# Memory norms inside the first keys' product, later probabilities: a two-layer decoder trunk on one core

## The chip, the cores and the metric

The kernel runs on one core of a Trainium2 chip. The metric is the device time of one execution in microseconds (us); the kernel before is timed at 556.08 us, the median of 3 runs (556.07 to 556.79).

## The reference, cut to what matters

Two layers (`DEPTH = 2`) of width 1024 work on 256 tokens (x) and 256 memory rows (mem), all in float32. Layer 0 mixes tokens with causal windows (`pool_mixer`), layer 1 with masked attention; each layer also lets the tokens attend to the memory with four heads of 64, joins both results in one output projection and ends with an MLP of width 4096.

```python
for i in range(DEPTH):
    u = rms_norm(x, g_mix[i])
    mem_n = rms_norm(mem, g_mem[i])
    ...                       # h = u @ w_in ; tok = pool_mixer(..) or moba_mixer(..) ; qm = last columns of h
    mo = mem_cross_attention(qm, mem_n, w_mem_kv[i], mem_q_gain[i], mem_k_gain[i])
    x = x + jnp.concatenate([tok, mo], axis=-1) @ w_out[i]
    u = rms_norm(x, g_mlp[i])
    x = x + jnp.square(jax.nn.relu(u @ w_ff1[i])) @ w_ff2[i]

def mem_cross_attention(qm, mem_n, w_mem_kv, q_gain, k_gain):
    k, v = jnp.split(mem_n @ w_mem_kv, 2, axis=-1)
    q = rms_norm(qm.reshape(B, S, MEM_HEADS, HEAD_DIM), q_gain)
    k = rms_norm(k.reshape(B, M, MEM_HEADS, HEAD_DIM), k_gain)
    ...
    p = jax.nn.softmax(s, axis=-1).astype(v.dtype)
    o = jnp.einsum('bhsm,bmhd->bshd', p, v)
```

## The kernel before, in words

**Products.** A float32 operand is split into a rounded part `hi` and a rest `lo`; `mm3` (L137 to L140) multiplies them in three matmuls: hi by hi, lo by hi, hi by lo. Weights come in blocks of 512 KB into one pool of seven buffers (`raw`, issued by SyncE in program order, L116). ScalarE makes `hi` (L131 with a gain, L127 without), VectorE makes `lo` (L134, L128). A transfer leaves when the buffer that it takes has been read.

**Stages of layer 0**, in order: the input projection; the memory's keys and values of layer 0, `aK = mem_kv_mm(0, ...)`, eight steps k = 0 to 7 over two accumulators (here called the first keys' product); inside it, at k = 5 (`PLAN['pool']`), the whole of `pooling`: four blocks of pool weights, the window products `band`, which ScalarE and VectorE turn into `d` (L145, L146), and the group products `group`, turned into the first six pieces of `cat`; then `aK1 = mem_kv_mm(1, ...)`, the keys and values of layer 1 (the second keys' product); then the output projection `wout_phase` over eight pieces of `cat`, in the order of `PLAN['wout0']`, four of them on four accumulators and the rest as a tail; then the residual sums and their transposes; then the MLP.

**The memory's part.** After the first keys' product both blocks of mem are loaded and squared (`norm_stats`, L177), and `rsqrt` takes the power on GpSimd (L184). A key block is finished by `head_r` (square L197, sum L199, epsilon L208, power L184), `kn` (L268), `mv` (L269), two transposes (L271) and `mkh`, `mkl`. `mem_scores` makes the scores of one block of 128 queries (L356), their maxima (L360) and exponents (L320), and VectorE divides by the sums (L331). `later` holds back the transposes of the probabilities (L337, L342) by `LAG = 2` steps; `flush` runs what is held; `av_out` (L377) multiplies probabilities and values into pieces 6 and 7 of `cat`. `PLAN['mem0']` says at which k of the second keys' product the steps stand: first key block, second key block, scores of block 0, scores of block 1.

**Order.** The order on each engine is made by a scheduler from dependencies and the program's order, and each engine runs its instructions in that order. Only some stretches are fixed by hand (`manual_schedule`), none of them where the change is. The accumulators are four PSUM banks (`acc`), the other products take turns in four more (`ps`).

Of the kernel before, what the change touches and what calls it, by code (L numbers as in the profile page):

```python
# [35 lines left out]
NWARM = 7  # L36
LAG = 2

PLAN = {'x': 6, 'q': 5, 'bw': 7, 'pool': 5, 'mem0': (2, 4, 6, 6),
        'mem1': (2, 4, 8, 5), 'tok': (5, 7, 8), 'out': 2,  # L40
        'bands': ((0, 2), (1, 1), (3, 5), (4, 4)), 'group': (2, 0, 4), 
        'wout0': (2, 4, 5, 6, 0, 1, 7, 3), 'wout1': (6, 7, 0, 2, 1, 3, 4, 5)}
B0 = P + 16


# [8 lines left out]
def trunk(ctx: ExitStack, tc: tile.TileContext, x, mem, x_t0, x_t, mem_t, small, bands, rope, mask,  # L54
# [13 lines left out]
    def nm(s):  # L68
        uid[0] += 1
        return f"{s}_{uid[0]}"  # L70
# [183 lines left out]

        return [head_r(a[b][:, :MEMW], 4, mem_e64[b], f"mk{b}") for b in range(2)], last_sum[0]

    def mem_kv_finish(l, a, kr, pool):

        kr, sums = kr
        hi = pool.tile([P, 2, S], F32R, tag="mkh", name=nm("mkh"))  # L260
        lo = pool.tile([P, 2, S], F32R, tag="mkl", name=nm("mkl"))
        v = pool.tile([P, 2, MEMW], F32, tag="mv", name=nm("mv"))
        ps = psum("mem_kv_finish")

        def block(b):
            kn = st.tile([P, MEMW], F32, tag="kn", name=nm("kn"))
            with tc.issue_after(sums.ins):
                nc.vector.tensor_tensor(heads(kn), heads(a[b][:, :MEMW]), bcast(kr[b], 4), op=ALU.mult)  # L268
            nc.scalar.activation(v[:, b, :], a[b][:, MEMW:], AF.Copy, scale=mem_r[b])  # L269
            for c in range(2):  # L270
                nc.tensor.transpose(ps[:, c * S + b * P:c * S + b * P + P], kn[:, c * P:(c + 1) * P], ident)  # L271

        def end():
            evac_split(ps.rearrange("p (c t) -> p c t", c=2), hi, lo, mgain[l])
            return hi, lo, v

        return [lambda: block(0), lambda: block(1), end]

    def mem_q(a, b, qT, hold=None):

# [63 lines left out]

        later(back)

    def mem_scores(b, mq, mk, a, pool, nbuf, put):

        ps = [psum("mem_scores") for _ in range(2)]
        for c in range(2):
            for i, (x, y) in enumerate(((0, 0), (0, 1), (1, 0))):
                for j in range(2):
                    rr = slice(j * HD, j * HD + HD)
                    nc.tensor.matmul(ps[j][:, c * S:(c + 1) * S], mq[x][rr, c, b * P:(b + 1) * P], mk[y][rr, c, :],  # L356
                                     start=i == 0, stop=i == 2)
        for j in range(2):
            mx = st.tile([P, 2], F32, tag="mx", name=nm("mx"), bufs=4)
            nc.vector.tensor_reduce(mx, ps[j].rearrange("p (h n) -> p h n", h=2), axis=AX.X, op=ALU.max)  # L360
            nb = st.tile([P, 2], F32, tag="nb", name=nm("nb"), bufs=4)
            nc.vector.scalar_tensor_tensor(nb, mx, -1.0, a[:, j:j + 3:2], op0=ALU.mult, op1=ALU.mult)
            p = pool.tile([P, 512], F32, tag="s", name=nm("s"), bufs=nbuf[0])
            exp_t(pool, [(ps[j][:, c * S:(c + 1) * S], S, a[:, 2 * c + j:2 * c + j + 1], nb[:, c:c + 1])
                         for c in range(2)], p, nbuf[1], lambda t, j=j: put(t, j))

# [10 lines left out]
                        nc.tensor.matmul(o[j * HD:j * HD + HD, cs], vv, pT, start=i == 0, stop=i == n - 1)  # L377
        evac_split(o.rearrange("p (c t) -> p c t", c=2), cat[0][:, c0:c0 + 2, :], cat[1][:, c0:c0 + 2, :])

    def mem_heads(cat, mq, mk, a, pool, nbuf):  # L380

        got = {}

        def scores(b):
            mem_scores(b, mq, mk[:2], a[b], pool, nbuf, lambda t, j: got.__setitem__((b, j), t))

        def gather():
            av_out(cat, 6, [[[(got[b, h % 2][:, (h // 2) * S + kb * P:(h // 2) * S + (kb + 1) * P],
                               mk[2][:, kb, h * HD:(h + 1) * HD]) for kb in range(2)]
                             for b in range(2)] for h in range(4)])  # L390

        return [lambda: scores(0), lambda: scores(1), lambda: later(gather)]
# [132 lines left out]
    with tc.tile_pool(name="l0", bufs=1) as lp:  # L525
# [111 lines left out]
            evac_split(ps.rearrange("p (c t) -> p c t", c=2), cat[0][:, co:co + 2, :], cat[1][:, co:co + 2, :])  # L637

        wpool = {}
        mid_hi = []  # L640

        def pooling():
            for b in range(2):
# [10 lines left out]
                band_pair(c0, c1)  # L654
            for co in PLAN['group']:
                group_pair(co)
            mid_hi.append(last_hi[0])


        mgain = []  # L660
        for l in range(2):
# [1 line left out]
            nc.vector.scalar_tensor_tensor(g, sm[:, MQG + l:MQG + l + 1], 8.0, sm[:, MKG + l:MKG + l + 1],  # L663
                                           op0=ALU.mult, op1=ALU.mult)
            mgain.append(g)
        aK = mem_kv_mm(0, [(PLAN['pool'], pooling)])
        mem_r, mem_e64 = [], []
        after = mid_hi[0]
        for b in range(2):
            raw = load_raw(mem[b * P:(b + 1) * P, :])  # L670
            ms = norm_stats(raw[:, 0, :], f"mem{b}", after)
            mem_r.append(rsqrt(ms, f"mem{b}"))
            mem_e64.append(scaled(ms, 64.0 * EPS, f"mem{b}"))
        kr = mem_kv_norm(aK)
        steps = []

        def mem_keys(i):
# [1 line left out]
                steps.extend(mem_kv_finish(0, aK, kr, lp))  # L679
            steps[i]()  # L680
            if i == 1:
                steps.extend(mem_heads(cat, mq, steps[2](), mqa, lp, (2, 4)))

        aK1 = mem_kv_mm(1, list(zip(PLAN['mem0'], [lambda: mem_keys(0), lambda: mem_keys(1),
                                                   lambda: steps[3](), lambda: steps[4]()])))
        steps[5]()
        flush()
        steps = mem_kv_finish(1, aK1, mem_kv_norm(aK1), mkp)
        mk1 = [step() for step in steps][2]
        x1T = big_t("x1T")  # L690
        after_mix(wout_phase(0, PLAN['wout0'], cat, PSC), x1T)


    x2T = big_t("x2T")
# [234 lines left out]
```

## Time and profile before

| | |
|---|---|
| median of 3 runs | 556.08 us |
| the profiled execution | 557.27 us |
| its span, first to last instruction | 555.5 us |
| TensorE (PE) busy | 545.8 us, 98% |
| VectorE (DVE) busy | 386.5 us, 70% |
| ScalarE (ACT) busy | 357.5 us, 64% |
| granted TensorE clock | 1.000 |

The span and every row below come from one profiled execution, whose time outside the span is 1.8 us. PE is TensorE's matrix products, DVE VectorE, ACT ScalarE, POOL GpSimd, SP SyncE. A row of the timeline gives start, length and work; the bracket at its end is the idle time ahead of it on that engine and who ended it. Products overlap: one of 512 columns is shown 0.39 us long, while the next starts 0.23 us after it. So a wait of TensorE is best read from the starts.

### The profile page before, as it was taken

The numbers are of one execution on the slowest core, as the hardware profiler recorded it, in microseconds if no ns is written. First come the engines' busy times: TensorE is split into PE (matmuls) and PEld (weight loads), VectorE is DVE, ScalarE is ACT, GpSimd is POOL, SyncE is SP. The second block draws the span as 40 slices with busy tenths as digits, with TensorE's granted clock in tenths as the row PEclk, the third lists the DMA queues.
The fourth block names the chain that finished last, engine by engine and source line by source line (L and its number), as shares of the span: only waits on it lengthen the run. The fifth ranks groups of instructions, "written<-read, shape, count | busy, mean of one in ns | idle before, by whom it ended". The sixth has DMA issues, their size and how long they took to land.

```text
span 555.5 us, 8204 instructions
## 1 busy us (share of the span) xinstructions
PE 545.8 (98%) x2883; PEld 456.8 (82%) x2883; DVE 386.5 (70%) x765; ACT 357.5 (64%) x658; POOL 43.7 (8%) x57
## 2 busy tenths in 40 slices
PE   8999899999999999999999999999999999999997
PEld 5888687888888888888888876888888888888885
DVE  5897978584864945848979988565858477485462
ACT  5888967756566566565769579757664665656510
POOL 0102100000000000000013365300000000000000
PEclk9999999999999999999999999999999999999999
DMA  8989674355737538458571444342574483663401
GB/s 283 353 255 345 229 239 136 105 196 213 226 129 250 178 138 291 124 181 264 168 233 65 158 152 151 116 152 77 183 272 137 167 281 101 225 208 140 145 0 76
DMA packets 46712, 101.94 MB, mean 184 GB/s; under 512 B 3664, under 2 KB 11600, under 8 KB 46672
## 3 DMA queue, kind: packets, MB, share of 16 engines
q1 hardware_dynamic: 46528, 101.42, 55.5%
q8 instruction: 22, 0.36, 0.3%
q14 instruction: 18, 0.15, 0.1%
q10 hardware_dynamic: 144, 0.01, 0.0%
HBM read 100.37 MB, written 1.05 MB: 183 GB/s over the span
## 4 chain that ended last, share of the span: by engine, by line
PE 85%; ACT 6%; DVE 4%; DMA 2%; POOL 2%; issue 1%; SPq 1%; ACTq 0%
PE step L462 18%; PE acc L139 16%; PE acc L138 16%; PE acc L140 16%; PE step L465 10%; PE acc L462 3%; ACT hi L131 2%; PE av_out L377 2%; ACT s L320 1%; PE acc L465 1%; DMA raw<-in_w_in_pool_dram 1%; DVE lo L134 1%; DMA raw<-in_w_mem_kv_dram 1%; POOL r L184 1%; PE exp_t L337 1%; PE transpose L157 1%
## 5 line engine op out<-in xcount | busy, mean ns | idle before, releaser
L131 ACT ACTIVATE hi<-raw,sm 128x512 fp32r<-128x512 f32 (+1 forms) x212 | 148.4, 722 | 53.3 <-PE acc L140 25.6
L134 DVE SCALAR_TENSOR_TENSOR lo<-raw,sm,hi 128x512 fp32r<-128x512 f32 x212 | 150.3, 749 | 19.0 <-ACT hi L131 18.2
L127 ACT ACTIVATE hi<-raw 128x512 fp32r<-128x512 f32 (+1 forms) x152 | 93.9, 630 | 73.8 <-PE acc L140 65.6
L138 PE MATMUL acc<-hi,hh 128*128 128x512 f32 x256 | 99.9, 390 | 0.0
L140 PE MATMUL acc<-hi,hl 128*128 128x512 f32 x256 | 99.8, 390 | 0.0
L139 PE MATMUL acc<-lo,hh 128*128 128x512 f32 x256 | 99.8, 390 | 0.0
L128 DVE TENSOR_TENSOR lo<-raw,hi 128x512 fp32r<-128x512 f32 (+1 forms) x152 | 96.4, 692 | 3.6 <-ACT hi L127 3.5
L446 DVE TENSOR_TENSOR r<-step,c 128x256 f32<-128x256 f32 x56 | 23.6, 421 | 98.6 <-ACT c L445 98.6
L140 PEld LDWEIGHTS acc<-hi,hl 128*128 128x128 f32 x256 | 48.1, 188 | 10.0
L138 PEld LDWEIGHTS acc<-hi,hh 128*128 128x128 f32 x256 | 48.1, 188 | 9.5
L139 PEld LDWEIGHTS acc<-lo,hh 128*128 128x128 f32 x256 | 48.1, 188 | 9.4
L462 PE MATMUL step<-x3T,hi 128*128 128x512 f32 x224 | 51.9, 389 | 0.0
L462 PE MATMUL step<-x1T,hi 128*128 128x512 f32 x224 | 51.9, 389 | 0.0
L462 PEld LDWEIGHTS step<-x3T,hi 128*128 128x128 f32 x224 | 42.0, 188 | 8.7
L462 PEld LDWEIGHTS step<-x1T,hi 128*128 128x128 f32 x224 | 42.0, 188 | 8.7
L445 ACT ACTIVATE c<-step 128x256 f32<-128x256 f32 x56 | 21.2, 379 | 19.5 <-PE step L465 19.5
L138 PE MATMUL acc<-hi,x2T 128*128 128x512 f32 x80 | 32.2, 403 | 0.0
L140 PE MATMUL acc<-hi,x2T 128*128 128x512 f32 x80 | 31.2, 391 | 0.0
L139 PE MATMUL acc<-lo,x2T 128*128 128x512 f32 x80 | 31.2, 391 | 0.0
L465 PEld LDWEIGHTS step<-x3T,lo 128*128 128x128 f32 x224 | 27.8, 192 | 0.5
L465 PEld LDWEIGHTS step<-x1T,lo 128*128 128x128 f32 x224 | 27.8, 192 | 0.5
L465 PE MATMUL step<-x3T,lo 128*128 128x256 f32 x224 | 28.0, 283 | 0.0
(152 smaller groups left out, 758.9 us busy)
## 6 DMA issues: line engine op xcount, KB each, us to landing
raw<-in_w_ff_dram SPq DMA_DIRECT2D x128, 512.0 KB, 4.8
raw<-in_w_out_dram SPq DMA_DIRECT2D x16, 512.0 KB, 4.9
raw<-in_w_in_moba_dram SPq DMA_DIRECT2D x24, 256.0 KB, 4.5
raw<-in_w_mem_kv_dram SPq DMA_DIRECT2D x8, 512.0 KB, 5.4
raw<-in_w_in_moba_dram SPq DMA_DIRECT2D x8, 512.0 KB, 5.0
raw<-in_w_in_pool_dram SPq DMA_DIRECT2D x6, 512.0 KB, 7.1
raw<-in_w_in_pool_dram SPq DMA_DIRECT2D x4, 256.0 KB, 4.5
xr<-in_x_dram SPq DMA_DIRECT2D x2, 512.0 KB, 7.5
```

Of the source, the lines that this page charges most:

```text
L127: nc.scalar.activation(hi, raw, AF.Copy)
L128: nc.vector.tensor_tensor(lo, raw, hi.bitcast(F32), op=ALU.subtract)
L131: last_hi[0] = nc.scalar.activation(hi[:, :m], raw[:, :m], AF.Copy, scale=g)
L134: nc.vector.scalar_tensor_tensor(lo, raw, g, hi.bitcast(F32), op0=ALU.mult, op1=ALU.subtract)
L138: nc.tensor.matmul(o, a[0], b[0], start=start, stop=False)
L139: nc.tensor.matmul(o, a[0], b[1], start=False, stop=False)
L140: nc.tensor.matmul(o, a[1], b[0], start=False, stop=stop)
L377: nc.tensor.matmul(o[j * HD:j * HD + HD, cs], vv, pT, start=i == 0, stop=i == n - 1)
L445: nc.scalar.activation(c, zs[i][:, S:], AF.Copy)
L446: nc.vector.tensor_tensor(z[:, i, :], zs[i][:, :S], c, op=ALU.add)
L462: nc.tensor.matmul(o, pieces[k][0][:, n * P:(n + 1) * P], t[2][:, k, :, :], start=k == 0, stop=False)
L465: nc.tensor.matmul(o[:, :S], pieces[k][1][:, n * P:(n + 1) * P], t[0][:, k, :], start=False, stop=k == NKC - 1)
```

## The change

The two blocks of mem are loaded and squared inside the first keys' product, at k = 4 (`mstat`), ahead of `pooling`, instead of after it. The steps of the first keys move from k = 2, 4, 6, 6 to k = 3, 3, 5, 5 of the second keys' product. Up to five held transposes may wait (`lag[0] = 5`), so that probabilities and values run between the pieces of the output projection, ahead of its pieces 1, 2 and 3 (`probs0`). The probabilities of block 1 stay in the buffers of `hhi` and `hlo` (`home`). The second keys are finished in two parts: `kn` and `mv` ahead of the output projection, the transposes after `av_out` (`apart`). The output projection takes the two pieces of `av_out` last.

```diff
-PLAN = {'x': 6, 'q': 5, 'bw': 7, 'pool': 5, 'mem0': (2, 4, 6, 6),
+PLAN = {'x': 6, 'q': 5, 'bw': 7, 'pool': 5, 'mstat': 4, 'mem0': (3, 3, 5, 5), 'probs0': (1, 2, 3),
...
-        'wout0': (2, 4, 5, 6, 0, 1, 7, 3), 'wout1': (6, 7, 0, 2, 1, 3, 4, 5)}
+        'wout0': (2, 4, 5, 0, 1, 3, 6, 7), 'wout1': (6, 7, 0, 2, 1, 3, 4, 5)}
...
-        ps = psum("mem_kv_finish")
+        ps = None if apart else psum("mem_kv_finish")
+        kns = []
...
             nc.scalar.activation(v[:, b, :], a[b][:, MEMW:], AF.Copy, scale=mem_r[b])
+            kns.append(kn)
+            if not apart:
+                turn(b)
+
+        def turn(b):
+            nonlocal ps
+            ps = ps or psum("mem_kv_finish")
             for c in range(2):
-                nc.tensor.transpose(ps[:, c * S + b * P:c * S + b * P + P], kn[:, c * P:(c + 1) * P], ident)
+                nc.tensor.transpose(ps[:, c * S + b * P:c * S + b * P + P], kns[b][:, c * P:(c + 1) * P], ident)
...
-        return [lambda: block(0), lambda: block(1), end]
+        return [lambda: block(0), lambda: block(1)] + [lambda: turn(0), lambda: turn(1)] * apart + [end]
...
-            p = pool.tile([P, 512], F32, tag="s", name=nm("s"), bufs=nbuf[0])
+            if home:
+                p = pool.tile([P, 2, TOK], F32, tag=home[j], name=nm("s"))[:, 0, :512]
+            else:
+                p = pool.tile([P, 512], F32, tag="s", name=nm("s"), bufs=nbuf[0])
...
-        aK = mem_kv_mm(0, [(PLAN['pool'], pooling)])
         mem_r, mem_e64 = [], []
-        after = mid_hi[0]
-        for b in range(2):
-            raw = load_raw(mem[b * P:(b + 1) * P, :])
-            ms = norm_stats(raw[:, 0, :], f"mem{b}", after)
-            mem_r.append(rsqrt(ms, f"mem{b}"))
-            mem_e64.append(scaled(ms, 64.0 * EPS, f"mem{b}"))
+
+        def mem_stats():
+            for b in range(2):
+                raw = load_raw(mem[b * P:(b + 1) * P, :])
+                ms = norm_stats(raw[:, 0, :], f"mem{b}")
+                mem_r.append(rsqrt(ms, f"mem{b}"))
+                mem_e64.append(scaled(ms, 64.0 * EPS, f"mem{b}"))
+
+        aK = mem_kv_mm(0, [(PLAN['mstat'], mem_stats), (PLAN['pool'], pooling)])
...
+        lag[0] = 5
         aK1 = mem_kv_mm(1, list(zip(PLAN['mem0'], [lambda: mem_keys(0), lambda: mem_keys(1),
                                                    lambda: steps[3](), lambda: steps[4]()])))
         steps[5]()
-        flush()
-        steps = mem_kv_finish(1, aK1, mem_kv_norm(aK1), mkp)
-        mk1 = [step() for step in steps][2]
+        steps = mem_kv_finish(1, aK1, mem_kv_norm(aK1), mkp, True)
+        steps[0](), steps[1]()
+        mk1 = []
+
+        def gather():
+            flush()
+            mk1.extend([step() for step in steps[2:]][2])
+
         x1T = big_t("x1T")
-        after_mix(wout_phase(0, PLAN['wout0'], cat, PSC), x1T)
+        after_mix(wout_phase(0, PLAN['wout0'], cat, PSC,
+                             list(zip(PLAN['probs0'], [lambda: flush(2), lambda: flush(2), gather]))), x1T)
+        lag[0] = LAG
```

The scheduler turns this into changes of order, shown at three places. In each row stand the line, the operation and output <- inputs.

First ScalarE, in the first keys' product, from the split of step k = 4 on. `raw_453` holds the weights of k = 4 and 5, `raw_600` those of k = 6 and 7, `raw_469` to `raw_487` are the pool weights, `d` comes from the bands. Before:

```order
L131 ACTIVATE hi_455<-raw_453,sm 128x512
L127 ACTIVATE hi_471<-raw_469 128x512
L127 ACTIVATE hi_477<-raw_475 128x512
L127 ACTIVATE hi_483<-raw_481 128x512
L127 ACTIVATE hi_489<-raw_487 128x256
L131 ACTIVATE hi_590<-raw_453,sm 128x512
L131 ACTIVATE hi_602<-raw_600,sm 128x512
L131 ACTIVATE hi_612<-raw_600,sm 128x512
L145 ACTIVATE d_402<-band_493 128x2x256
L145 ACTIVATE d_402<-band_506 64x256
L145 ACTIVATE d_402<-band_516 128x2x256
```

Of the change (`raw_455` and `raw_466` are mem, `raw_491` to `raw_509` the pool weights, `raw_622` the weights of k = 6 and 7):

```order
L131 ACTIVATE hi_477<-raw_453,sm 128x512
L177 ACTIVATE junk_457,m_458<-raw_455 128x1024
L177 ACTIVATE junk_468,m_469<-raw_466 128x1024
L127 ACTIVATE hi_493<-raw_491 128x512
L127 ACTIVATE hi_499<-raw_497 128x512
L145 ACTIVATE d_402<-band_515 128x2x256
L127 ACTIVATE hi_505<-raw_503 128x512
L127 ACTIVATE hi_511<-raw_509 128x256
L145 ACTIVATE d_402<-band_528 64x256
L145 ACTIVATE d_402<-band_538 128x2x256
L131 ACTIVATE hi_612<-raw_453,sm 128x512
L131 ACTIVATE hi_624<-raw_622,sm 128x512
```

The two squares stand ahead of the pool weights, and the split of k = 5 (`hi_590` before, `hi_612` now) has moved from ahead of the three evacuations of the bands to behind them.

Second TensorE, from the last band product to the first group products (`acc_407` and `acc_408` are the first keys' accumulators). Before:

```order
L611 MATMUL band_516<-bw_254,hlo 128x128
L138 MATMUL acc_407<-hi_590,mth 128x512
L139 MATMUL acc_407<-lo_591,mth 128x512
L140 MATMUL acc_407<-hi_590,mtl 128x512
L138 MATMUL acc_408<-hi_590,mth 128x512
L139 MATMUL acc_408<-lo_591,mth 128x512
L140 MATMUL acc_408<-hi_590,mtl 128x512
L138 MATMUL acc_407<-hi_602,mth 128x512
L139 MATMUL acc_407<-lo_603,mth 128x512
L138 MATMUL group_539<-d_402,hi_477 128x256
```

Of the change:

```order
L624 MATMUL band_538<-bw_254,hlo 128x128
L138 MATMUL acc_407<-hi_612,mth 128x512
L138 MATMUL acc_408<-hi_612,mth 128x512
L138 MATMUL group_561<-d_402,hi_499 128x256
L138 MATMUL group_576<-d_402,hi_493 128x256
L139 MATMUL group_576<-d_402,hi_493 128x256
```

Between bands and groups there were eight products, now two, and both need the split of k = 5.

Third the end of the second keys, on VectorE up to `kn` of both blocks. Before:

```order
L324 RECIPROCAL inv_825<-sums_822 128x2
L128 TENSOR_TENSOR lo_1041<-raw_1034,hi_1040 128x512
L331 TENSOR_SCALAR s_821<-s_821,inv_825 128x256 x2
L199 TENSOR_REDUCE ss_899<-sq_897 128x4
L134 SCALAR_TENSOR_TENSOR lo_1047<-raw_1044,sm,hi_1046 128x512
L208 TENSOR_SCALAR sst_901<-ss_899,s_642 128x4
L268 TENSOR_TENSOR kn_909<-acc_660,r_895 128x256
L268 TENSOR_TENSOR kn_914<-acc_661,r_903 128x256
```

Of the change:

```order
L340 TENSOR_SCALAR s_790<-s_790,inv_794 128x256 x2
L333 RECIPROCAL inv_806<-sums_803 128x2
L199 TENSOR_REDUCE ss_844<-sq_842 128x4
L340 TENSOR_SCALAR s_802<-s_802,inv_806 128x256 x2
L208 TENSOR_SCALAR sst_846<-ss_844,s_464 128x4
L199 TENSOR_REDUCE ss_852<-sq_850 128x4
L128 TENSOR_TENSOR lo_1037<-raw_1034,hi_1036 128x512
L208 TENSOR_SCALAR sst_854<-ss_852,s_475 128x4
L270 TENSOR_TENSOR kn_861<-acc_660,r_848 128x256
L270 TENSOR_TENSOR kn_864<-acc_661,r_856 128x256
```

`kn` of the second keys stands behind all four scaled probabilities (`s_752` to `s_802`) as before; two splits fewer stand between them. On TensorE of the change, from the transposes of the last probabilities on:

```order
L346 MATMUL exp_t_930<-ident,s_790 128x128 x4
L346 MATMUL exp_t_937<-ident,s_802 128x128 x3
L138 MATMUL acc_870<-hi_874,cat_401 128x512
L139 MATMUL acc_870<-lo_875,cat_401 128x512
L140 MATMUL acc_870<-hi_874,cat_401 128x512
```

`acc_870`, the third accumulator of the output projection, is the bank of the second keys' `acc_660`; its first product now follows the transposes of the probabilities at once, where before `av_out` and the second keys' transposes stood between.

## Rows read from the trace of the kernel before

**Rows 1.** The page's part 1: busy time, share of the span, instructions of each engine.

```profile
PE 545.8 (98%) x2883; PEld 456.8 (82%) x2883; DVE 386.5 (70%) x765; ACT 357.5 (64%) x658; POOL 43.7 (8%) x57
```

**Rows 2.** Stretches: length, busy PE, PEld, DVE, ACT, POOL, clock, DMA share, GB/s.

```profile
52.00:66.00 14.00, 12.07 (x71) 9.20 (x71) 12.87 (x30) 13.05 (x28) 1.47 (x2) 1.00 0.83 298
78.00:100.00 22.00, 22.00 (x105) 17.83 (x104) 14.30 (x25) 15.17 (x26) 0.00 (x0) 1.00 0.60 191
```

**Rows 3.** Timeline of TensorE, 51 to 66 us: start, length, work, [idle before <- releaser].

```profile
51.76 0.39 PE L140 MATMUL acc<-hi,mtl 128*128 128x512 f32 x1
52.56 0.44 PE L271 MATMUL mem_kv_finish<-ident,kn 128*128 128x128 f32 x2 [0.41 <-DVE kn L268]
...
58.68 0.38 PE L356 MATMUL mem_scores<-mkh,mqh 64*128 64x256 f32 x2
59.28 0.39 PE L356 MATMUL mem_scores<-mkl,mqh 64*128 64x256 f32 x2 [0.21 <-DVE mkl L149]
...
63.41 0.39 PE L140 MATMUL acc<-hi,mtl 128*128 128x512 f32 x1
65.11 0.63 PE L337 MATMUL exp_t<-ident,s 128*128 128x128 f32 x4 [1.31 <-DVE s L331]
```

**Rows 4.** Timeline of TensorE, 39 to 47 us, bands to the end of the groups.

```profile
39.18 0.45 PE L611 MATMUL band<-bw,hlo 128*128 128x128 f32 x3
...
40.04 0.45 PE L138 MATMUL acc<-hi,mth 128*128 128x512 f32 x1
...
41.94 0.40 PE L138 MATMUL group<-d,hi 128*128 128x256 f32 x2
...
46.97 0.40 PE L140 MATMUL acc<-hi,mtl 128*128 128x512 f32 x1
```

**Rows 5.** Timeline of ScalarE, 34 to 74 us.

```profile
34.62 1.97 ACT L127 ACTIVATE hi<-raw 128x512 fp32r<-128x512 f32 x4
...
39.44 1.40 ACT L145 ACTIVATE d<-band 128x512 fp32r<-128x512 f32 x3 [1.01 <-PE band L611]
...
43.39 1.34 ACT L131 ACTIVATE hi<-raw,sm 128x512 fp32r<-128x512 f32 x2 [1.72 <-DMA raw<-in_w_mem_kv_dram]
...
48.65 1.06 ACT L177 ACTIVATE junk<-raw 128x1024 bf16<-128x1024 f32 x1
...
49.70 0.39 ACT L197 ACTIVATE sq<-acc 128x256 f32<-128x256 f32 x1
...
73.34 0.47 ACT L269 ACTIVATE mv<-acc,r 128x256 f32<-128x256 f32 x1 [0.75 <-DVE kn L268]
```

**Rows 6.** Timeline of VectorE, 53 to 80 us.

```profile
53.50 0.42 DVE L268 TENSOR_TENSOR kn<-acc,r 128x256 f32<-128x256 f32 x1 [1.00 <-POOL r L184]
...
61.00 1.28 DVE L360 TENSOR_REDUCE mx<-mem_scores 128x2 f32<-128x512 f32 x2
...
66.19 1.41 DVE L134 SCALAR_TENSOR_TENSOR lo<-raw,sm,hi 128x512 fp32r<-128x512 f32 x2
...
71.55 0.22 DVE L208 TENSOR_SCALAR sst<-ss,s 128x4 f32<-128x4 f32 x1
...
75.60 4.08 DVE L134 SCALAR_TENSOR_TENSOR lo<-raw,sm,hi 128x512 fp32r<-128x512 f32 x6
```

**Rows 7.** Timeline of GpSimd, 52 to 68 us.

```profile
52.46 1.01 POOL L184 TENSOR_TENSOR r<-sst,mhalf 128x4 f32<-128x4 f32 x1
66.36 1.44 POOL L184 TENSOR_TENSOR r<-sst,mhalf 128x4 f32<-128x4 f32 x1 [12.89 <-DVE sst L208]
```

**Rows 8.** DMA issues at 15.9, 28.4 and 33.1 us: count, KB each, us to landing.

```profile
raw<-in_mem_t_dram SPq DMA_DIRECT2D x1, 256.0 KB, 8.5
...
raw<-in_w_pool_pad_dram SPq DMA_DIRECT2D x1, 256.0 KB, 3.4
...
raw<-in_w_mem_kv_dram SPq DMA_DIRECT2D x1, 512.0 KB, 3.5
```

More of the change, by code (lines that the diff above doesn't have):

```diff
@@ L255, in mem_kv_norm, with mem_kv_finish @@
         return [head_r(a[b][:, :MEMW], 4, mem_e64[b], f"mk{b}") for b in range(2)], last_sum[0]
-    def mem_kv_finish(l, a, kr, pool):
+    def mem_kv_finish(l, a, kr, pool, apart=False):
         kr, sums = kr
@@ L345, in exp_t, with mem_scores @@
         later(back)
-    def mem_scores(b, mq, mk, a, pool, nbuf, put):
+    def mem_scores(b, mq, mk, a, pool, nbuf, put, home=None):
         ps = [psum("mem_scores") for _ in range(2)]
@@ L378, in av_out, with mem_heads @@
         evac_split(o.rearrange("p (c t) -> p c t", c=2), cat[0][:, c0:c0 + 2, :], cat[1][:, c0:c0 + 2, :])
-    def mem_heads(cat, mq, mk, a, pool, nbuf):
+    def mem_heads(cat, mq, mk, a, pool, nbuf, home=None):
         got = {}
         def scores(b):
-            mem_scores(b, mq, mk[:2], a[b], pool, nbuf, lambda t, j: got.__setitem__((b, j), t))
+            mem_scores(b, mq, mk[:2], a[b], pool, nbuf, lambda t, j: got.__setitem__((b, j), t), home if b else None)
         def gather():
@@ L639, in trunk @@
         wpool = {}
-        mid_hi = []
         def pooling():
@@ L656, in pooling @@
                 group_pair(co)
-            mid_hi.append(last_hi[0])
         mgain = []
@@ L681, in mem_keys @@
             if i == 1:
-                steps.extend(mem_heads(cat, mq, steps[2](), mqa, lp, (2, 4)))
+                steps.extend(mem_heads(cat, mq, steps[2](), mqa, lp, (2, 4), ('hhi', 'hlo')))
+        lag[0] = 5
         aK1 = mem_kv_mm(1, list(zip(PLAN['mem0'], [lambda: mem_keys(0), lambda: mem_keys(1),
```

## The prediction

> **What bounds the kernel now.** I read the page's busy times first: TensorE works 98% of the span [rows 1]. So its arithmetic stands, and a change of order can only take away or add waits of TensorE. The stretches say where: from 52 to 66 us it is busy 12.07 of 14 us, while ScalarE and VectorE are nearly full with 13.05 and 12.87; from 78 us on it is never idle and the other two have room [rows 2]. Whatever TensorE loses ahead of 78 us therefore comes out at the end unshortened.
>
> Next I read TensorE's own timeline, by starts. Back to back, a product of 512 columns follows the last after 0.23 us, one of 256 after 0.12: the 42 group products take 46.97 - 41.94 = 5.03 us [rows 4]. Against these spacings TensorE loses three pieces in the stretch that the change touches [rows 3]: 52.56 - 51.76 - 0.23 = 0.57 us for `kn` of the first keys, 59.28 - 58.68 - 0.12 = 0.48 for `mkl`, and 65.11 - 63.41 - 0.23 = 1.47 for the first scaled probabilities. Together 2.5 us. That is all there is to win.
>
> **The change part by part.** All of it is counted from the order on each engine of the changed kernel with lengths of rows of before. Up to 34.62 us, where the split of k = 4 is done, both orders agree.
>
> *Squares moved, 2 x 1.05 us.* A square holds ScalarE from 48.65 to 49.70 [rows 5]. Two of them leave the full stretch and go to where ScalarE has idle time of 1.01 and 1.72 us [rows 5]. Their two VectorE operations each and their powers on GpSimd go along, beside other work, and cost TensorE nothing. The loads of mem go past the four pool weights and the weights of k = 6, 7 on SyncE's queue. The first now takes the place of the pool weights at 28.4 us, and with the bytes ahead of it I put its landing between 3.5 and 6 us later (a lone block of its size took 3.5 [rows 8]), so before ScalarE wants it at 34.62. The weights of k = 6, 7 wait for the buffer of the first square: 34.62 + 1.2 = 35.8 instead of 33.1, landing at 39.3 by the same 3.5; wanted at 42.2 (below). So far the move is free.
>
> *The wait that the move makes.* ScalarE runs in order. After the squares (to 36.7) it splits two pool blocks at 0.52 each (four, the last half as wide, in 1.97 less the overlap [rows 5]) and is ready at 37.8. The next in its order is the first `d`, which needs the last band products. These start on TensorE at 39.18, behind step k = 4 [rows 4], and nothing moves them: `d` starts at 39.44 as now [rows 5]. Behind it stand two pool blocks (0.83 us) and two more pieces of `d`; the three pieces take 1.40 less an overlap of 0.1 [rows 5]. So the split of k = 5 starts at 39.44 + 1.30 + 0.83 = 41.57, and is to be seen 0.76 later, at 42.33 (0.73 long [rows 5], and a hop). TensorE wants it at 40.04, when the bands are done [rows 4]: **a new wait of 2.29 us**. Before, that split ran ahead of the bands' evacuations. TensorE then has two products, to 42.79, and the groups need the last piece of `d`, which now stands behind the split of k = 6: 41.57 + 2 x 0.61 (two splits in 1.34 [rows 5]) + 0.4 = 43.2, **0.41 more**. Groups begin at 43.2 instead of 41.94, and with only 2 of 8 products done ahead of them; TensorE is 2.70 us late.
>
> *First keys, scores, first probabilities.* Groups to 48.23, then ten products of k = 5, 6 and three of k = 7 (13 x 0.23): the first keys' square starts at about 51.4 and, with the 4.2 us from square to second `kn` of now (49.70 [rows 5] to 53.92 [rows 6]), the second `kn` is there at 55.6. TensorE has 34 products first, to 56.05: the wait of 0.57 is gone, with 0.45 to spare. Transposes and two steps bring it to 59.3. VectorE does five splits at 0.67 (six in 4.08 [rows 6]) and `mkl` after 55.6, ready at 59.7: 0.2 us of the 0.48 stay, counting the pair that needs only `mkh`. Scores to 61.05, then 24 products that now stand between scores and probabilities, to 66.6; VectorE has the maxima from 55.6 + 9 x 0.67 = 61.6 on and the first probabilities at 65: the wait of 1.47 is gone. This part does what it says. `home` costs nothing: `hhi` and `hlo` were last read by the bands. The order of the pieces of `wout0` changes no count.
>
> *Second keys.* On TensorE the transposes of the probabilities end at 66.6 + 15 x 0.11 (a group of four is 0.63 long less an overlap of 0.2 [rows 3]) + 6 x 0.23 = 69.65. Then comes the third accumulator, in the bank that the second keys' `mv` must empty; `av_out`, which covered that before, comes later. VectorE took 71.55 - 61.00 = 10.55 us from the first maxima to the second keys' last epsilon, with hardly a break [rows 6]; up to the first of the two, four splits (2.6) and one sum (0.3) less stand there now, 7.6 us: 69.2. Then a power on GpSimd (1.01 [rows 7], with hops 1.1), `kn` (0.42 [rows 6]) and `mv` (0.47 [rows 5]): 71.3. **A new wait of 1.65 us.** Bounds: another power took 1.44, at 66.36, beside splits of VectorE [rows 6, 7], which makes 2.1; and the twelve splits of VectorE on this path at 0.60 instead of 0.67 make 0.85. I take the middle, since at 69.2 VectorE waits for the power soon after. What follows (`av_out`, second transposes) has its inputs early.
>
> On GpSimd's 1.44 us the Trainium skill (SBUF — State Buffer, section "SBUF: two separate sides") says that GpSimd and VectorE lock one shared port pair, for a whole instruction when VectorE reads two SBUF inputs. The splits at 66.19 are such instructions and the trace agrees with 1.44 against 1.01 [rows 6, 7]; by the rule the power would be long here too, and the sum 0.4 us larger.
>
> *The sum.* New 2.29 + 0.41 + 1.65, gone 0.57 + 0.28 + 1.47: 4.35 - 2.32 = +2.0 us. The profiled execution of 557.27 us would become 559.3; it lies 1.2 above the median of the runs shown, so the median goes from 556.08 to **558.1**. The bounds of the last wait alone give 557.3 to 558.5.
>
> **The rivals.** *The wait at the second keys is hidden.* If VectorE is faster on this path (this count has it busy nearly without a break from 42 to 71 us), or TensorE loses more on the way, the third accumulator is free in time and only 2.70 - 2.32 = 0.4 us are left: 556.5, up to 557.1 with half of it. For it: it hangs on a chain of some 30 us; against: four powers and evacuations in a row, none of which can overlap.
>
> *Not slower: the bands end earlier.* It hangs on one place: when the first `d` can start. All that I count behind it, on ScalarE, VectorE and TensorE alike, moves with it one for one, down to the 37.8 at which ScalarE is ready. If the bands' last products ran ahead of step k = 4 on TensorE, `d` would start 1.64 us earlier and the time would be 558.1 - 1.6 = 556.5; from a `d` at 38.5 on it is no longer slower by what can be measured. Only with the hidden second wait on top, 1.65 less, is it faster, 554.8. Against it: both orders have the bands' last products behind k = 4, and TensorE reaches them unhindered at 39.18 [rows 4].
>
> *Slower still: mem lands late.* Loads issued into a full queue took up to 8.5 us [rows 8]. So late, mem would be there at 36.9; two squares and two pool blocks then end at 40.1 instead of 37.8, the first `d` slips by 0.7 and the weights of k = 6, 7 by 2.3, to 41.6, just in time. Some 0.7 to 1 us more: 559.0.
>
> **How the numbers follow.** The forecast 0.57; the hidden second wait 0.23; bands earlier 0.12, of which 0.06 with the second wait hidden too; late mem 0.08. The range for 8 in 10 runs from 556.4 (just under the two cases at 556.5) to 559.1; outside it lie the faster case and what goes beyond late mem. A measurement here can tell about 0.2%, 1.1 us, from no change: faster than 555.0 has 0.06, within 0.2% 0.23 + 0.06 = 0.29, and slower than 557.2 has 0.57 + 0.08 = 0.65.
>
> **What would show it.** In the changed kernel's trace TensorE should wait about 2.3 us for ScalarE's split of weights at 40 us, behind the bands; then 0.4 for a `d`; nothing for `kn` and for the first probabilities; 0.2 for `mkl`; and 0.9 to 2.1 us for `mv` of the second keys at about 70 us. From the second piece of the output projection on it should be as full as before. If the first wait is under 1 us I am wrong about the order's worth; if the waits stand and the time is still below 557, the later stages give something back that I count as nothing.

## The result and the profile after

The changed kernel takes 559.97 us (median of 4 runs, 559.92 to 559.98), the kernel before 556.21 in the same comparison: a ratio of 1.0066, 95% interval 1.0053 to 1.0079. It is slower, as forecast, but by 3.76 us and not by 2.0, and 559.97 lies above the range of 556.4 to 559.1. The profiled execution took 559.98, with a span of 557.9.

The page's busy times answer [rows 1], and the two stretches answer [rows 2] (columns as there):

```profile
PE 547.0 (98%) x2883; PEld 457.8 (82%) x2883; DVE 387.1 (69%) x765; ACT 357.8 (64%) x658; POOL 42.9 (8%) x57
```

```profile
52.00:66.00 14.00, 13.91 (x79) 11.23 (x79) 13.15 (x30) 11.13 (x24) 2.03 (x2) 1.00 0.68 231
78.00:100.00 22.00, 22.00 (x131) 17.81 (x129) 15.37 (x26) 14.22 (x24) 0.00 (x0) 1.00 0.51 161
```

From 52 to 66 us TensorE is now busy 13.91 of 14 us, against 12.07: of the three waits ahead of `kn`, `mkl` and the first probabilities only a part of the one for `mkl` is left (below), and ScalarE has fallen from 13.05 to 11.13. The loss must stand elsewhere. TensorE's list of waits from 24 to 110 us (total, times, longest) has two new long ones:

```profile
PE acc L138 <- ACT hi L131: 2.1, 1, 2.1
PE acc L138 <- ACT mv L271: 1.4, 1, 1.4
PE group L138 <- ACT d L145: 0.3, 1, 0.3
```

TensorE's timeline behind the bands answers [rows 4]; here every row counts by its start:

```profile
38.68 0.45 PE L624 MATMUL band<-bw,hlo 128*128 128x128 f32 x3
...
39.43 0.27 PE L624 MATMUL band<-bw,hlo 128*128 128x128 f32 x1
41.77 0.73 PE L138 MATMUL acc<-hi,mth 128*128 128x512 f32 x2 [2.06 <-ACT hi L131]
42.78 0.79 PE L138 MATMUL group<-d,hi 128*128 128x256 f32 x2 [0.28 <-ACT d L145]
43.38 0.41 PE L139 MATMUL group<-d,hi 128*128 128x256 f32 x1
43.59 0.41 PE L140 MATMUL group<-d,lo 128*128 128x256 f32 x1
...
45.94 0.31 PE L140 MATMUL group<-d,lo 128*128 128x256 f32 x1
46.09 0.28 PE L138 MATMUL group<-d,hi 128*128 128x256 f32 x1
46.20 0.28 PE L139 MATMUL group<-d,hi 128*128 128x256 f32 x1
...
49.32 0.40 PE L139 MATMUL acc<-lo,mth 128*128 128x512 f32 x1
```

The wait stands where the forecast put it. But look at the products after it: up to 45.94 a group product follows the last after 0.21 us, from 46.09 on after 0.12. The 42 of them take 49.32 - 42.78 = 6.54 us instead of 5.03. The stretches' clock column (third from the right) says why:

```profile
40.00:42.00 2.00, 0.23 (x1) 0.24 (x2) 2.00 (x5) 2.00 (x6) 0.00 (x0) 1.00 0.99 354
42.00:44.00 2.00, 1.72 (x7) 1.28 (x7) 1.94 (x5) 1.95 (x5) 0.00 (x0) 0.65 1.03 398
44.00:46.00 2.00, 2.00 (x12) 2.00 (x11) 2.00 (x4) 1.32 (x3) 0.00 (x0) 0.50 1.03 382
46.00:48.00 2.00, 2.00 (x19) 2.00 (x19) 0.73 (x3) 1.36 (x3) 0.00 (x0) 1.00 0.94 363
```

TensorE is busy for only 0.23 us between 40 and 42 us. Behind that the granted clock falls to 0.50, the 1.2 GHz level, and stays there until 46 us; the 0.65 belongs to a stretch that holds both levels. The kernel before kept 1.00 there:

```profile
42.00:44.00 2.00, 2.00 (x19) 2.00 (x18) 0.32 (x1) 0.61 (x1) 0.00 (x0) 1.00 1.04 398
44.00:46.00 2.00, 2.00 (x19) 2.00 (x18) 1.82 (x3) 1.98 (x5) 0.00 (x0) 1.00 1.06 401
```

The rest of TensorE's timeline, at the places of [rows 3]:

```profile
56.82 0.39 PE L140 MATMUL acc<-hi,mtl 128*128 128x512 f32 x1
57.06 0.60 PE L280 MATMUL mem_kv_finish<-ident,kn 128*128 128x128 f32 x4
...
60.36 0.38 PE L366 MATMUL mem_scores<-mkh,mqh 64*128 64x256 f32 x2
60.83 0.39 PE L366 MATMUL mem_scores<-mkl,mqh 64*128 64x256 f32 x2
...
67.68 0.39 PE L140 MATMUL acc<-hi,cat 128*128 128x512 f32 x1
67.91 1.03 PE L346 MATMUL exp_t<-ident,s 128*128 128x128 f32 x8
68.70 0.48 PE L138 MATMUL acc<-hi,cat 128*128 128x512 f32 x1
...
70.16 0.93 PE L346 MATMUL exp_t<-ident,s 128*128 128x128 f32 x7
72.51 0.50 PE L138 MATMUL acc<-hi,cat 128*128 128x512 f32 x1 [1.42 <-ACT mv L271]
```

`kn` and the first probabilities come 0.24 and 0.23 us behind the product ahead of them, which is no wait. `mkl` still costs 60.83 - 60.36 - 0.12 = 0.35. Eight transposes took 0.79, so seven end the work at 70.85, and the third accumulator starts at 72.51: 1.66 us lost.

ScalarE around the first wait, for [rows 5]:

```profile
34.13 1.04 ACT L177 ACTIVATE junk<-raw 128x1024 bf16<-128x1024 f32 x1
...
35.29 1.06 ACT L177 ACTIVATE junk<-raw 128x1024 bf16<-128x1024 f32 x1
...
38.94 0.60 ACT L145 ACTIVATE d<-band 128x512 fp32r<-128x512 f32 x1 [1.45 <-PE band L624]
39.43 0.93 ACT L127 ACTIVATE hi<-raw 128x512 fp32r<-128x512 f32 x2
40.26 0.84 ACT L145 ACTIVATE d<-band 64x256 fp32r<-64x256 f32 x2
41.00 1.33 ACT L131 ACTIVATE hi<-raw,sm 128x512 fp32r<-128x512 f32 x2
42.35 0.38 ACT L145 ACTIVATE d<-band 64x256 fp32r<-64x256 f32 x1
```

The squares run at 34.13 and 35.29 without a wait, so mem is there in time. ScalarE then idles 1.45 us in front of the first `d`, while the split that TensorE will miss stands two pool blocks and two `d` behind it, at 41.00.

**A measure for what follows.** The time from the start to the first band product moves from one execution to the next, in these profiles from 28.46 to 29.40 us, and so do short waits in the second layer. Where kernels are compared by trace, I take the stretch from the first band product to the first memory scores of the second layer. Its two ends, before and then after:

```profile
29.22 0.97 PE L607 MATMUL band<-bw,hhi 128*128 128x256 f32 x4
...
288.53 0.38 PE L356 MATMUL mem_scores<-mkh,mqh 64*128 64x256 f32 x2
```

```profile
28.72 0.97 PE L620 MATMUL band<-bw,hhi 128*128 128x256 f32 x4
...
291.42 0.38 PE L366 MATMUL mem_scores<-mkh,mqh 64*128 64x256 f32 x2
```

It is 288.53 - 29.22 = 259.31 us before and 291.42 - 28.72 = 262.70 after: +3.39. Each of these values is that of one profiled execution.

### The profile page after: what moved, and what is told of

It is laid out like the page before. It is cut to its first block, busy times and chain, and to the rows that moved or that the text cites. A ratio compares the mean times of both kernels' runs of the same rounds, so it can differ in the third digit from the quotient of the medians.

```text
span 557.9 us, 8199 instructions
## 1 busy us (share of the span) xinstructions
PE 547.0 (98%) x2883; PEld 457.8 (82%) x2883; DVE 387.1 (69%) x765; ACT 357.8 (64%) x658; POOL 42.9 (8%) x57
## 4 chain that ended last, share of the span: by engine, by line
PE 84%; ACT 7%; DVE 5%; DMA 1%; issue 1%; POOL 1%; SPq 1%; ACTq 0%; DVEq 0%
PE step L475 18%; PE acc L139 16%; PE acc L138 16%; PE acc L140 16%; PE step L478 10%; PE acc L475 3%; ACT s L329 2%; DVE lo L134 2%; ACT hi L131 2%; PE acc L478 1%; PE av_out L390 1%; DMA raw<-in_w_in_pool_dram 1%; PE transpose L157 1%; ACT hi L127 1%; POOL r L184 1%
```

## The experiments

My theory after the result, **A**: the order makes both waits as forecast, and the rest is the clock, which falls behind the first wait. The rival, **B**: the group products are slow for a reason of their own, such as late operands or splits beside them. The experiments ran in three groups on three chips, each beside the kernel before: its medians were 556.44 us (e1_fill to e4_stats6), 556.55 (e5_after to e8_ahead) and 556.39 (e9_fill to e12_only). Each ratio is against the kernel before of the same group.

**The wait filled (e1_fill).** Ten products of a zero tile behind the bands, in an accumulator that is empty then (it is the one that the second keys' product takes next; the lines that pass it on are left out):

```
             for c0, c1 in PLAN['bands']:
                 band_pair(c0, c1)
+            kv1.extend([accum(), accum()])
+            for _ in range(NFILL):
+                nc.tensor.matmul(kv1[0], warm[:, :P], warm, start=True, stop=True)
```

> The changed kernel with ten products of a zero tile (128x512, bf16, the tile of the warm-up) put on TensorE right behind the band products, in an accumulator that is empty then. They fill the 2.1 us in which TensorE waits there for the split of k = 5; the wait for the split itself, and every other engine's order, stay. Theory A (the idle time costs twice: the forecast left out that the granted clock falls behind it, to 0.50 from 44 to 46 us): the clock reads 1.00 from 40 to 48 us, the 42 group products take about 5.0 us instead of 6.54, the two products of k = 5 take 0.23 each, and the time falls by 1.75 us to 558.2 (557.9 to 558.5). Theory B (the group products are slow for another reason: their operands come late, or they compete for a memory with splits that now run beside them): the clock or not, they still take about 6.5 us and the time stays at 559.9 to 560.1.

Measured 559.46 us, ratio 1.0056 (1.0043 to 1.0069). Two stretches of its trace:

```profile
42.00:44.00 2.00, 1.72 (x9) 0.90 (x8) 1.94 (x5) 1.95 (x4) 0.00 (x0) 1.00 1.04 395
44.00:46.00 2.00, 2.00 (x19) 2.00 (x18) 2.00 (x4) 2.00 (x4) 0.00 (x0) 1.00 1.07 386
```

The clock stays at 1.00 and the groups take 48.60 - 43.46 = 5.14 us, with the same splits beside them. B falls. The stretch measure is 261.40, 1.30 under the changed kernel and +2.09 over the kernel before, which is the forecast's sum of 2.0. My 1.75 was too much: it counted the pair of products of k = 5 as slow, but that pair is 0.73 us long in both traces, and the groups start 14.06 us behind the first band in both, since they wait for `d` anyway. The time of 558.2 was missed too: this profile reaches the bands 0.68 us later, and it came from another chip than the result.

**The norms' move undone (e2_late).** The two squares go behind the pooling again:

```
-        aK = mem_kv_mm(0, [(PLAN['mstat'], mem_stats), (PLAN['pool'], pooling)])
+        aK = mem_kv_mm(0, [(PLAN['pool'], pooling)])
+        mem_stats()
...
-                ms = norm_stats(raw[:, 0, :], f"mem{b}")
+                ms = norm_stats(raw[:, 0, :], f"mem{b}", mid_hi[0])
```

> The changed kernel with the one move of the memory's norms undone: the squares stand behind the pooling again, as in the kernel before; the keys' and scores' new places and the probabilities between the output projection's products stay. Theory A: no wait of TensorE behind the bands, the clock 1.00 throughout, groups 5.0 us, which is 2.1 + 0.3 + 1.75 = 4.2 us back; of that about 0.4 is lost to kn of the first keys (squares late again, transposes one step later than before) and up to 1 to a longer wait at the second keys, whose chain on VectorE cannot be pulled forward as far as TensorE: 556.7 (556.0 to 557.5). Theory B (the lost time has nothing to do with the norms' place or with the idle behind it): 558.2 or more.

Measured 556.67 us, ratio 1.0010 (1.0001 to 1.0019), 259.08 by the stretch. No wait behind the bands, clock 1.00. So the whole loss hangs on the norms' move. What is left of the change is worth little either way: 0.1% more time, 0.23 us less by the stretch. It ends the wait for `kn`, shortens the one for the probabilities from 1.31 to 0.62, and makes a new one of 0.95 at the second keys. The 0.4 for `kn` did not come; the 0.62 for the probabilities was not expected.

**The norms' move alone (e3_only).** The kernel before, with its squares taken to step 4 of the first keys' product:

```
-        aK = mem_kv_mm(0, [(PLAN['pool'], pooling)])
...
+        aK = mem_kv_mm(0, [(PLAN['mstat'], mem_stats), (PLAN['pool'], pooling)])
```

> The kernel before with the one move of the memory's norms into the first keys' product; all else as before. Theory A: TensorE waits 2.1 and 0.3 us behind the bands and the clock falls to about 0.5 for some 3.5 us, as in the changed kernel (+4.2); the waits for kn (0.57) and part of mkl (0.3) go, the wait for the first scaled probabilities stays at 1 to 1.5, and there is none at the second keys: 556.2 + 4.2 - 0.9 - 0.2 = 559.3 (558.6 to 559.8), slower than before although it makes but one of the two new waits. Theory B: the wait alone, without the clock, 557.5.

Measured 560.28 us, ratio 1.0072 (1.0057 to 1.0087), 262.82 by the stretch: 1.0 us above the 559.3 expected, and 0.5 above the range. Its waits are 2.06 for the split, 0.18 for `d`, 1.4 for the probabilities and none at the second keys. The clock falls here as well:

```profile
42.00:44.00 2.00, 1.82 (x9) 1.48 (x8) 1.94 (x4) 1.95 (x5) 0.00 (x0) 0.50 1.06 405
44.00:46.00 2.00, 2.00 (x13) 2.00 (x13) 1.75 (x3) 1.06 (x2) 0.00 (x0) 0.65 1.05 411
```

**The norms two steps later (e4_stats6), and the split of k = 5 ahead (e8_ahead).** Both keep the norms inside the first keys' product and change only what stands ahead of the first `d` on ScalarE. The first is one number:

```
-PLAN = {'x': 6, 'q': 5, 'bw': 7, 'pool': 5, 'mstat': 4, 'mem0': (3, 3, 5, 5), 'probs0': (1, 2, 3),
+PLAN = {'x': 6, 'q': 5, 'bw': 7, 'pool': 5, 'mstat': 6, 'mem0': (3, 3, 5, 5), 'probs0': (1, 2, 3),
```

The second writes that split ahead of the pooling:

```
+                p = split(raw[:, j, :], sm[:, gcol + k:gcol + k + 1]) if k == ahead else None
                 for at, fn in hooks:
                     if at == k:
                         fn()
-                p = split(raw[:, j, :], sm[:, gcol + k:gcol + k + 1])
+                p = p or split(raw[:, j, :], sm[:, gcol + k:gcol + k + 1])
```

> The changed kernel with one number other: the norms are asked for at step 6 of the first keys' product instead of step 4. By the order on ScalarE the split of k = 5 and the first of k = 6 then stand ahead of the first band's evacuation, and the squares between and behind the evacuations. Theory A: TensorE has nine products behind the bands at once, waits under 0.5 us for the last piece of d, keeps its clock at 1.00, and the first keys' norms still come in time; the wait at the second keys stays or grows to 2.5 us: 559.97 - 4.2 + 0.4 + 0.5 = 556.7 (555.8 to 557.3). Theory B: 558.2 or more.

> The changed kernel with one thing other: the split of k = 5 is written ahead of the pooling, so that it stands ahead of the squares and of the bands' evacuations on ScalarE; the squares stay where the change put them. Theory A (it is the order on ScalarE, and not the squares' length, that makes the first wait, and the clock falls only for so long a wait): six products run behind the bands, then a wait of 0.5 to 0.8 us for the split of k = 6, groups start 0.9 us later than before instead of 2.7 behind, the clock stays at 1.00, and the second wait stays at 1.5: 259.3 to 259.9 us from the first band product to the second layer's scores, 556.8 (556.2 to 557.6) in all. Theory B (the squares' 2.1 us come out on TensorE wherever the split stands): 261.4 or more, and 558.5.

e4_stats6: 556.92 us, ratio 1.0013 (1.0003 to 1.0023), 258.88 by the stretch, and only the second wait left. e8_ahead: 556.57 us, ratio 1.0001 (0.9992 to 1.0009), 259.19. Its row behind the bands:

```profile
41.80 0.73 PE L138 MATMUL acc<-hi,mth 128*128 128x512 f32 x2 [0.63 <-ACT hi L131]
```

Six products run first, then 0.63 us are waited, and the groups start 13.62 us behind the first band, 0.90 later than the 12.72 of before, as worked out. The squares run in their new place at the same length. So it is their order against one split, and not their 2.1 us, that costs most of the time. The second wait was 0.79 here, not 1.5, and 0.35 for `kn` came back.

**The second wait: another bank (e6_bank), another order (e7_mv).** Both with the norms at step 6. In e6_bank the third and fourth accumulator of the first output projection come from the other pool:

```
-        a = [[accum(), accum()], [accum(), accum()]]
+        a = [[accum(), accum()], [psum('w'), psum('w')] if l == 0 else [accum(), accum()]]
```

> Norms asked for at step 6 (as in e4_stats6), and the third and fourth accumulator of the first output projection taken from the other PSUM pool, so that they no longer need the banks of the second keys. Theory A (the second new wait is the release of that bank by mv, as the forecast has it): the wait of 1.4 to 1.6 us before the third accumulator is gone; up to 0.6 may come back, since these two banks now hang on the exponentials of the first scores: 257.3 to 258.0 us from the first band product to the second layer's scores, and 555.0 (554.4 to 555.9) in all, faster than before. Rival (TensorE is held there by VectorE and ScalarE as a whole, whatever bank it writes): the wait only moves to the next instruction that needs a probability or the values: 258.9 and 556.8.

Measured 555.44 us, ratio 0.9978 (0.9968 to 0.9988): faster than both kernels. The one wait that is left between 24 and 110 us:

```profile
PE exp_t L346 <- ACT pT L351: 0.7, 1, 0.7
```

By the stretch 257.72: the 1.58 of e4_stats6 are gone and 0.71 came back, as a wait for a bank of the other pool. These two account for 0.87 of the 1.16 us between the stretches; the rest lies in small gaps. The rival, by which the wait only moves and the stretch stays at 258.9, falls: the second wait is the release of a bank.

e7_mv copies `mv` out ahead of `kn`:

```
+        if apart:
+            for b in range(2):
+                nc.scalar.activation(v[:, b, :], a[b][:, MEMW:], AF.Copy, scale=mem_r[b])
+
         def block(b):
...
-            nc.scalar.activation(v[:, b, :], a[b][:, MEMW:], AF.Copy, scale=mem_r[b])
+            if not apart:
+                nc.scalar.activation(v[:, b, :], a[b][:, MEMW:], AF.Copy, scale=mem_r[b])
```

> Norms at step 6, and the second keys' mv copied out ahead of their kn instead of behind it (mv needs only the memory's norms, and stood behind kn because that read the bank first). Theory A: the third accumulator is free when the first kn is done, some 0.5 us earlier: a wait of 1.0 to 1.1 instead of 1.58, 258.4 us from the first band product to the second layer's scores, and 556.3 (555.8 to 556.9) in all. If kn is delayed by as much as mv gains, nothing changes: 258.9, 556.8.

Measured 556.88 us, ratio 1.0005 (0.9994 to 1.0017), 259.30 by the stretch: theory A missed, and the time is that of its second case. The wait was 1.55, now for `kn` itself, and 0.33 us came up for `kn` of the first keys. VectorE had begun a split just ahead of the power, and the power took 1.44 us instead of 1.01 in e4_stats6 (rows in the last section), about as much as the 0.47 of `mv` that no longer stands in the chain. So the chain to `kn` now holds the bank. What the place of `mv` is worth by itself this run does not show, since two things changed in it.

**Fill and no fill on one chip (e9_fill to e12_only).** The times of e1_fill and the result came from two chips, so both pairs stand here once more together: e9_fill is e1_fill and e10_after the changed kernel, e11_only_fill is e3_only with the same fill and e12_only is e3_only.

> e1_fill once more, now on one chip with the changed kernel (e10_after), since their times so far came from two chips. Theory A, resized by the first traces (groups 5.14 us instead of 6.54 and 6.28, so 1.1 to 1.4 us): 1.1 to 1.4 us below e10_after, clock 1.00 from 40 to 48 us. Theory B: within 0.4 us of it.

> The changed kernel, the mark for e9_fill: 559.5 to 560.6 us, a granted clock of 0.5 to 0.65 between 42 and 46 us, 42 group products in 6.2 to 6.6 us.

> e3_only (the kernel before with the norms' move alone) with the same ten products behind the bands. Theory A: the same 1.1 to 1.4 us below e12_only as e9_fill is below e10_after, and the clock 1.00. Theory B: within 0.4 us of it. What then is left above the kernel before, some 2.4 us, is the price of the waits themselves.

> e3_only once more, the mark for e11_only_fill: 559.8 to 560.6 us, a granted clock of 0.5 to 0.65 between 42 and 46 us.

e11_only_fill took 559.06 us, e12_only 560.72: 1.66 between them, 261.71 and 263.13 by the stretch. That is A, a little larger than expected. But e9_fill took 559.02 and e10_after, the changed kernel itself, 558.69 (ratio 1.0043, 1.0030 to 1.0056). It waits as always, but its clock did not fall in the profile, nor by the mean clock in any of its five executions:

```profile
41.52 0.74 PE L138 MATMUL acc<-hi,mth 128*128 128x512 f32 x2 [2.07 <-ACT hi L131]
```

```profile
40.00:42.00 2.00, 0.48 (x2) 0.30 (x2) 2.00 (x6) 2.00 (x5) 0.00 (x0) 1.00 0.97 345
42.00:44.00 2.00, 1.72 (x14) 1.47 (x13) 1.94 (x4) 1.95 (x5) 0.00 (x0) 1.00 0.97 353
44.00:46.00 2.00, 2.00 (x19) 2.00 (x19) 1.97 (x4) 1.98 (x4) 0.00 (x0) 1.00 1.02 383
```

The same program with the same wait, at clock 1.00: its groups take 5.14 us, and the stretch 261.39, the filled kernels' value (261.40, and 261.46 in e9_fill). The expectation for e9_fill and e10_after was wrong, but the result and e10_after show the clock's price in one program: 262.70 - 261.39 = 1.3 us. They also show that where the clock holds anyway, filling the wait gains nothing (559.02 against 558.69). In e5_after, the changed kernel on the second chip, the clock fell again:

> The changed kernel once more, beside the others on one chip, as the mark for them. Between the first band product and the first memory scores of the second layer, which leaves out how long the start takes (it moved by 0.9 us between the profiles so far), its trace showed 262.7 us, the kernel before 259.3, and the kernel with the filled wait 261.4. Theory A and B: 262.7 again and a time of 559.5 to 560.3; a granted clock of 0.5 to 0.65 between 42 and 46 us.

It took 560.52 us, ratio 1.0068 (1.0052 to 1.0084), 262.50 by the stretch, with its groups in 6.28 us.

So whether the clock falls behind this wait varies between executions. A timed execution shows it by the mean clock of its span: 0.996 or 0.997 where it fell, 0.998 to 1.000 otherwise. With the wait open (the result, e3_only, e5_after, e10_after, e12_only) it fell in 18 of 26 executions; with the wait filled (e1_fill, e9_fill, e11_only_fill) in none of 15; in the kernel before in none of 58. The price shows within one run too: the two executions of e3_only that kept their clock took 559.13 and 559.22 us, the four others 560.23 to 562.20. What decides in a single execution is open. The start of the bands by itself does not, since e3_only fell with bands at 28.46 us and e10_after did not with bands at 28.47; nor does the chip, since e12_only fell in all five executions beside e10_after.

## Why the prediction was wrong in size

By its own steps, losses of TensorE in us by starts:

| step | forecast | the changed kernel's trace |
|---|---|---|
| wait for the split of k = 5 | 2.29 | 2.23 (41.77, due 0.11 behind the last band's start at 39.43) |
| last piece of `d` | 0.41 | 0.55 (42.78 - 41.77 - 0.46) |
| 42 group products behind the wait | not in the sum | 1.51 (6.54 - 5.03); 1.40 of it is the clock (6.54 - 5.14 in e10_after) |
| `kn` of the first keys | -0.57 | -0.57 |
| `mkl` | -0.28 | -0.13 |
| first probabilities | -1.47 | -1.47 |
| third accumulator | 1.65 | 1.66 |

**The step that failed is "What bounds the kernel now".** It read the stretch as arithmetic that "stands", to which an order "can only take away or add waits". So the sum priced an idle TensorE at the length of the idle time, and the granted clock behind it at nothing, without a reason. Here idle time of 2.06 us was followed by a fall of the clock in 18 of 26 executions, and the 42 products behind it then took 6.28 to 6.63 us in the four profiles that show it, against 5.14 at clock 1.00: 1.1 to 1.5 us more. The table's sum of 3.8 is 0.4 over the measured stretch. Of that 0.3 is `av_out`, which the forecast took as unchanged: by starts its 32 products take 2.21 us before and 1.89 after. The rest lies in small gaps that I have not followed.

**Right: the waits and their places, and their sizes within 0.15 us.** The groups came 14.06 - 12.72 = 1.34 us later and with six products of 0.24 still to do behind them, which is 2.8 late against 2.70 in the forecast. e10_after, e1_fill and e9_fill are the forecast's case without the clock: +2.1 us by the stretch, and 558.69 us in e10_after, inside the range. That 2.1 meets the sum of 2.0 so closely is in part luck: `d`, `mkl` and the groups cost 0.1 us or a little more each beyond the forecast, and `av_out` gave 0.3 back. So is the 1.65, the middle of 0.85 to 2.1: with other things changed ahead of it the same wait was 0.79 in e8_ahead and 1.58 in e4_stats6. The end of the result lies another 0.4 us above the stretch's +3.39; time outside the span makes 0.3 between the two profiles (559.98 - 557.9 against 1.8), and the start and the second layer's waits vary by as much.

**Right: what was free.** The loads of mem came in time (5.6 us to landing, inside the 3.5 to 6), the weights of k = 6, 7 too, no wait of TensorE shows for `home` or for the order of the output projection's pieces, and from 78 us on TensorE is full [rows 2]. That a loss ahead of 78 us comes out unshortened holds: the 1.40 us between no fill and fill at the groups (6.54 - 5.14) are still 1.30 at the second layer's scores.

**The rivals.** The second wait was not hidden, mem was not late, and the bands did not come earlier than step k = 4 allows. The rival that was missing is the clock.

**Slips that moved the sum by 0.1 us at most.** The terms of the second keys' chain add up to 71.2, not 71.3. Half of the second wait would leave 556.1 + 0.4 + 0.8 = 557.3, not 557.1. And the two squares did not leave the stretch from 52 to 66 us: they stood at 48.65 [rows 5] and 49.96, ahead of it.

**The power on GpSimd.** At the second keys the two powers took 2.07 us together (they start at 70.47), near the short price that I took, though a split of VectorE with two SBUF inputs started at 70.63. The Trainium skill's rule (SBUF — State Buffer, "SBUF: two separate sides"), that the shared port pair belongs to whichever starts first, agrees for the power, which had started first. Its other half, that the one that comes second is blocked, does not show: the split that started under the power took 0.68 us, as splits of its kind do elsewhere (0.67 to 0.69). By reading the rule as a matter of which instructions stand nearby I would have added 0.4 us that did not come.

## What to carry to other kernels

When an edit opens a wait on TensorE, price not only its length but what the granted clock does behind it: read the clock column of the stretch after the wait, in several executions, since the same wait was followed by a slow clock in 18 of 26 of them and then cost 1.1 to 1.5 us more. When work is moved ahead on an engine that runs in order, look for the instruction that waits there for another engine, and put what that engine needs next ahead of it: here one number, or one split written earlier, took back nearly all of the loss (556.92 and 556.57 us). A buffer taken from another pool can take a wait away where a reordered chain to its release does not: together with that number it made 555.44 us, 0.22% (0.12 to 0.32%) faster than the kernel before.

## What the runs showed of the hardware that I had not expected

**The granted clock, level by level.** Behind 2.06 us without a product it fell to the 1.2 GHz level in four of five profiles, not while TensorE idled but in the stretches after work had resumed, between 42 and 48 us, and came back there under full load. It also falls at times in kernels with shorter waits alone: e4_stats6 and e7_mv, whose longest waits are 1.58 and 1.55 us at the second keys, have mean clocks of 0.995 or 0.996 in 3 of 12 executions each, with 557.73 to 559.11 and 557.99 to 559.17 us against medians of 556.92 and 556.88. The profiled execution was not one of these, so where it fell is not shown, nor that this wait is the cause: e1_fill and e9_fill have the same wait with 1.54 and 1.53 us, and their clock fell in none of 10. In kernels whose waits are all under 1 us it did not fall: e2_late (0.95 as its longest) and e8_ahead (0.79) in none of 12 each, e6_bank (0.71) in none of 8.

**A power that starts under a running split is longer.** GpSimd, then VectorE, of e7_mv:

```profile
66.62 1.44 POOL L184 TENSOR_TENSOR r<-sst,mhalf 128x4 f32<-128x4 f32 x1 [13.47 <-DVE sst L208]
```

```profile
66.44 0.75 DVE L134 SCALAR_TENSOR_TENSOR lo<-raw,sm,hi 128x512 fp32r<-128x512 f32 x1
67.10 0.42 DVE L199 TENSOR_REDUCE ss<-sq 128x4 f32<-128x256 f32 x1
```

And of e4_stats6:

```profile
66.88 2.13 POOL L184 TENSOR_TENSOR r<-sst,mhalf 128x4 f32<-128x4 f32 x2 [13.47 <-DVE sst L208]
```

```profile
66.70 0.42 DVE L199 TENSOR_REDUCE ss<-sq 128x4 f32<-128x256 f32 x1
67.03 0.75 DVE L134 SCALAR_TENSOR_TENSOR lo<-raw,sm,hi 128x512 fp32r<-128x512 f32 x1
```

In e7_mv the power starts while a split runs and takes 1.44 us; in e4_stats6 it starts beside a reduction and takes 1.01 (the row holds two powers of 1.01 us, 0.1 apart), though a split follows 0.15 us later, and that split is as long (0.75) as the other. The power of 1.44 in [rows 7] started 0.17 us into the splits of [rows 6], too. So it is what runs at the power's start that counts. The 14 traces agree without an exception: seven powers of this size started under a running split of VectorE with two inputs in SBUF and took 1.44 to 1.52 us; the 105 others took 1.01 to 1.08, among them 14 that started under a running `hlo<-acc,r,hhi`, one of whose inputs lies in PSUM. An order in which VectorE goes from the epsilon straight to a split makes the power behind it 0.4 to 0.5 us longer.
